# Two strided value groups formed together in seven half-sized products, in a hybrid decoder layer on one core

## The chip, the cores and the metric

The kernel runs on one core of one Trainium2 chip. The metric is the device time of one execution in microseconds (us); below, TensorE is the matrix engine (PE in the profile, PEld its weight loads), VectorE is DVE, ScalarE is ACT, GpSimd is POOL and SyncE is SP. Engines run their own instruction streams strictly in order and wait for each other by semaphores. DMAs are issued by SP (loads of weights) and by POOL (sums of weights in DRAM, and small loads).

## The reference

One decoder layer on 512 tokens of width 1024. An input projection gives queries, keys and values for three token mixers; the branches are gated, merged, projected and normalised, and an MLP with a gated per-layer embedding follows. The part that the change touches is the value projection of the third mixer, dilated attention, with three groups of four heads of width 128:

```python
DIL_PAIRS = ((128, 1), (512, 4), (2048, 16))          # (window, dilation)
proj = x @ w_in                                       # dl_v: 1536 columns, 512 for each group
...
def to_strided(a):
    a = jnp.pad(a, ((0, 0), (0, Lp * dilation - S), (0, 0), (0, 0)))
    a = a.reshape(B, Lp, dilation, H, dh).transpose(0, 2, 3, 1, 4)
    return a.reshape(B, dilation, H, nb, n, dh)
...
o = jnp.einsum('brhcqk,brhckd->brhcqd', prob.astype(vb.dtype), vb)
```

Groups 1 and 2 (dilations 4 and 16) read keys and values by stride. In the kernel both are worked residue by residue modulo 4: residue c holds the 128 tokens c, c+4, c+8, ... (group 2 masks what is not a multiple of 16 away). So their values are wanted in four tiles of 128 tokens by residue.

## The kernel before

**Number format.** Every large product is taken in three passes on float32 data: an operand is split into a high half (a cast on ScalarE) and a low half (the rest, a subtraction on VectorE), and TensorE adds high x high, high x low and low x high. In mm3 (lines 86 to 89) and in v_items (lines 340 to 342) that is three matmuls for each 128-deep slice k.

**Blocks.** Weights come in blocks of 128x1024 (512 KB). fill (line 163) issues their loads on SP into seven raw buffers (`raw`); split_next (line 198) casts a block into `wh` (line 212) and subtracts into `wl` (line 214). RING = 7 (line 135) is the number of split blocks that can stand ready; a block's buffer comes free when the products that read it are done. pump runs this ahead of the products.

**Items.** The program is a list of items, one PSUM bank of products each (`mm`) with an evacuation (`ev`). main_order (line 36) sets their order; the loop at line 1658 walks it: before an item it evacuates the one before, pumps blocks, calls step, which advances the attention generators (sb_head, dil_head, da_block) by a stage, and lets sum_steps issue some DMAs. A scheduler then sets the final order on each engine from these dependencies; the streams shown below as "order" are its result.

**Values of the strided groups.** v_items (line 329) makes a group's 512 columns of values: four items, one for each 128 consecutive tokens, x as the stationary operand (the weights of a load), the weight block as the moving one, 8 slices k x 3 = 24 matmuls each. Groups 1 and 2 were in line at head index 1. Their results are copied into two borrowed raw blocks, and 32 transfers on SP (line 367) gather every fourth row into tiles by residue; after LAND = 6 steps they are handed to the heads.

**Heads.** dil_head, one for each head slot: logits of group 0 (line 1496) and of the strided groups (line 1512), table sums with a running maximum on VectorE (lines 1499 and 1520), exponentials on ScalarE (1505, 1527), a small exchange of maxima and denominators between token order and residue order (r0 and r1, folds at lines 1537 and 1539, sel to mxx), scaling (1561, 1565), transposes (1577, 1586), and the products with the values (1598, 1603). Heads 0 and 1 start one behind the other during the value items.

**Half-sized products elsewhere.** The gate and MLP products already use seven products of halved operands instead of eight. Sums of their weight blocks are formed in DRAM by POOL's DMAs, eight steps a set (up_steps, line 806; plain copy 825, adding copy 823), four sets in turn, from item 16 on at a rate of 1.6 steps an item. Sums of x for the gates are formed by mixer_forms (line 408).

Of the kernel before, what the change touches and what calls it, by code (L numbers as in the profile page):

```python
# [10 lines left out]
F32 = mybir.dt.float32  # L11
# [7 lines left out]
P = 128  # L19
# [16 lines left out]
def main_order():  # L36
# [19 lines left out]
def trunk(tc, a, out):  # L56
    nc = tc.nc
    es = ExitStack()
    with es:
# [7 lines left out]
        NSLOT = 42  # L67
# [67 lines left out]
        RING, RAW = 7, 7  # L135
# [184 lines left out]
        by = {}  # L320
        LAND = 6

        def by_residue(g):
            for _ in range(LAND):
                yield
            for c in range(4):
                V["dl_v", g, c] = by[g][c]

        def v_items(nv, name, g):
            blocks = [{"src": None, "w": 1024, "uses": 2, "own": False} for _ in range(2)]  # L330
            if name == "dl_v" and g > 0:
                items[-2]["blocks"] = blocks
            cs = [chunk(a["wv"][nv, c].rearrange("p k n -> p (k n)"), 1024) for c in range(4)]
            for tt in range(4):
# [11 lines left out]
                def ev(ps, tt=tt):  # L346
# [8 lines left out]
                    elif g == 0:  # L355
# [3 lines left out]
                    else:  # L359

                        b = blocks[tt // 2]
                        t = b["raw"][:, (tt % 2) * 512:(tt % 2) * 512 + 512]
                        cp(t, ps)
                        if tt == 0:
                            by[g] = [slot(name) for _ in range(4)]
                        for c in range(4):
                            nc.sync.dma_start(by[g][c][32 * tt:32 * tt + 32, :], t[c::4, :])
                        b["uses"] -= 1
                        if tt == 3:
                            pending.append(by_residue(g))  # L370
# [5 lines left out]
        for kind, name, j in order[2:]:  # L376
# [5 lines left out]
            else:  # L382
                v_items(nv, name, j)
# [17 lines left out]
        HB = slice(0, 256)  # L401
        HC = slice(256, 512)
# [5 lines left out]
        def mixer_forms():  # L408

            r = {}  # L410
            for h in range(2):
                for th in range(2):
                    for kp in range(2):
                        t = slot("xr")
                        i = nc.gpsimd.dma_start(t.rearrange("p (k t) -> p k t", k=2),
                                                xt[:, 4 * h + 2 * kp:4 * h + 2 * kp + 2, 256 * th:256 * th + 256])
# [1429 lines left out]
```

## Time and profile before

| | us |
|---|---|
| median of 3 runs (1063.29 to 1063.46) | 1063.42 |
| the profiled execution | 1063.83 |
| its span, from first to last instruction | 1062.1 |
| TensorE busy in it | 1050.6 |
| VectorE busy | 750.0 |
| ScalarE busy | 558.5 |

How to read it: a busy share is an average over stages with different limits. Matmuls overlap, so the duration of one in the profile is longer than the distance from its start to the next one's start; the latter is what a matmul costs in a stream. A row of a timeline shows start, duration, engine, line, operation, output<-inputs, shape and count, and in brackets how long the engine was idle before and what released it. A row of a window table shows the stretch, its length, then the busy time (and number of instructions) of TensorE, its weight loads, VectorE, ScalarE and POOL, the granted TensorE clock, the DMA engines' share and their GB/s.

### The profile page before, as it was taken

To read this page: it belongs to the slowest core of one execution; us is meant where nothing else is said; L and a number is where in the kernel's file an instruction comes from. 1 tells how busy PE (TensorE), PEld (TensorE's weight loads), DVE (VectorE), ACT (ScalarE), POOL (GpSimd) and SP (SyncE) were. 2 spreads that over 40 slices of the span, in tenths; PEclk is the share of its full clock that TensorE was granted. 3 is DMA by queue.
4 is the path that set the end of the run, shared out by engine and by line. 5 is a ranking of instruction groups with operands and counts; after the bars stand their busy time and mean duration, and the time that the engine had idled before them with its cause. 6 is when DMAs were issued, how large, how long until landed. Compare 5 with 4: busy or idle time off the path is not lost.

```text
span 1062.1 us, 15599 instructions
## 1 busy us (share of the span) xinstructions
PE 1050.6 (99%) x5826; PEld 904.5 (85%) x5826; DVE 750.0 (71%) x1345; ACT 558.5 (53%) x975; POOL 130.1 (12%) x200
## 2 busy tenths in 40 slices
PE   9999999999999999999999999999999999999996
PEld 6888788888888888888999988888999989989885
DVE  6888667548253757768777773888777877877965
ACT  6666545525232546547545452675766665665741
POOL 0000402021121102230111030101110010000000
PEclk9999999999999999999999999999999999999999
DMA  8433656395896819773766583149989688867502
GB/s 314 134 130 99 210 149 168 140 297 135 315 245 193 235 38 316 153 244 98 200 180 202 175 290 137 67 138 268 269 282 276 235 239 255 259 229 244 189 14 79
DMA packets 60987, 208.21 MB, mean 196 GB/s; under 512 B 7944, under 2 KB 8856, under 8 KB 60912
## 3 DMA queue, kind: packets, MB, share of 16 engines
q1 hardware_dynamic: 37728, 125.76, 34.0%
q0 software_dynamic: 22608, 80.55, 29.4%
q8 instruction: 45, 0.74, 0.3%
q10 hardware_dynamic: 576, 0.92, 0.2%
q14 instruction: 30, 0.25, 0.1%
HBM read 202.97 MB, written 73.42 MB: 260 GB/s over the span
## 4 chain that ended last, share of the span: by engine, by line
PE 88%; DVE 7%; issue 2%; ACT 2%; DMA 0%; POOL 0%; SPq 0%; DVEq 0%; POOLq 0%
PE mm L87 13%; PE mm L89 13%; PE mm L88 13%; PE at L87 4%; PE at L983 4%; PE at L984 4%; PE at L985 4%; PE at L88 4%; PE at L89 4%; PE mm L340 3%; PE mm L342 3%; PE mm L341 3%; DVE wl L214 2%; PE at L131 1%; PE at L312 1%
## 5 line engine op out<-in xcount | busy, mean ns | idle before, releaser
L212 ACT CAST wh<-raw 128x1024 fp32r<-128x1024 f32 (+1 forms) x243 | 250.5, 1034 | 253.7 <-PE mm L88 154.5
L214 DVE TENSOR_TENSOR wl<-raw,wh 128x1024 fp32r<-128x1024 f32 (+1 forms) x243 | 291.5, 1205 | 109.8 <-ACT wh L212 106.4
L87 PE MATMUL mm<-xhT,wh 128*128 128x512 f32 x368 | 146.8, 399 | 0.0
L89 PE MATMUL mm<-xhT,wl 128*128 128x512 f32 x368 | 144.4, 392 | 0.0
L88 PE MATMUL mm<-xlT,wh 128*128 128x512 f32 x368 | 144.1, 392 | 0.0
L89 PEld LDWEIGHTS mm<-xhT,wl 128*128 128x128 f32 x368 | 69.1, 188 | 15.0 <-DVE wl L214 0.3
L87 PEld LDWEIGHTS mm<-xhT,wh 128*128 128x128 f32 x368 | 69.2, 188 | 13.6 <-issue 0.4
L88 PEld LDWEIGHTS mm<-xlT,wh 128*128 128x128 f32 x368 | 69.2, 188 | 13.1
L983 PE MATMUL at<-wh,hh 128*128 128x512 f32 x188 | 73.7, 392 | 0.0
L984 PE MATMUL at<-wl,hh 128*128 128x512 f32 x188 | 73.7, 392 | 0.0
L87 PE MATMUL mm<-x1hT,wh 128*128 128x256 f32 x256 | 73.6, 288 | 0.0
L985 PE MATMUL at<-wh,hl 128*128 128x512 f32 x188 | 73.1, 389 | 0.0
L88 PE MATMUL mm<-x1lT,wh 128*128 128x256 f32 x256 | 72.3, 283 | 0.0
L89 PE MATMUL mm<-x1hT,wl 128*128 128x256 f32 x256 | 71.8, 283 | 0.0
L340 PE MATMUL mm<-wh,xhT 128*128 128x512 f32 x160 | 63.4, 396 | 0.0
L342 PE MATMUL mm<-wh,xlT 128*128 128x512 f32 x160 | 62.5, 391 | 0.0
L341 PE MATMUL mm<-wl,xhT 128*128 128x512 f32 x160 | 62.4, 390 | 0.0
L823 POOL DMA_DIRECT2D usum<-in_wu_dram x32 | 28.0, 874 | 232.8 <-DVE wl L214 199.4
L87 PEld LDWEIGHTS mm<-x1hT,wh 128*128 128x128 f32 x256 | 48.8, 190 | 4.7 <-ACT up L917 2.7
L88 PEld LDWEIGHTS mm<-x1lT,wh 128*128 128x128 f32 x256 | 48.8, 191 | 1.5
L89 PEld LDWEIGHTS mm<-x1hT,wl 128*128 128x128 f32 x256 | 48.6, 191 | 0.0
L823 POOL DMA_DIRECT2D dsum<-in_wd_dram x28 | 26.1, 930 | 139.1 <-DVE wl L214 134.8
(437 smaller groups left out, 2538.4 us busy)
## 6 DMA issues: line engine op xcount, KB each, us to landing
usum<-in_wu_dram POOLq DMA_DIRECT2D x48, 512.0 KB, 8.8
raw<-in_wt_dram SPq DMA_DIRECT2D x46, 512.0 KB, 5.7
dsum<-in_wd_dram POOLq DMA_DIRECT2D x42, 512.0 KB, 9.1
raw<-usum SPq DMA_DIRECT2D x32, 512.0 KB, 6.4
raw<-dsum SPq DMA_DIRECT2D x28, 512.0 KB, 4.7
raw<-in_wd_dram SPq DMA_DIRECT2D x25, 512.0 KB, 4.4
raw<-in_wu_dram SPq DMA_DIRECT2D x24, 512.0 KB, 6.1
raw<-in_wv_dram SPq DMA_DIRECT2D x20, 512.0 KB, 5.0
```

The source lines that it names most:

```text
L87: nc.tensor.matmul(ps, wh, xh, start=start, stop=False, skip_group_check=True)
L88: nc.tensor.matmul(ps, wh, xl, start=False, stop=False, skip_group_check=True)
L89: nc.tensor.matmul(ps, wl, xh, start=False, stop=stop, skip_group_check=True)
L212: i = nc.scalar.copy(h, raw)
L214: i = nc.vector.tensor_sub(lo, raw, h.bitcast(F32))
L340: nc.tensor.matmul(ps, x1, c["h"][:, s], start=k == 0, stop=False)
L341: nc.tensor.matmul(ps, x1, c["l"][:, s], start=False, stop=False)
L342: nc.tensor.matmul(ps, x2, c["h"][:, s], start=False, stop=k == 7)
L823: i = nc.gpsimd.dma_start(o, i, accum_op=OP.add, max_dma_last_dim=4096)
L983: nc.tensor.matmul(ps, h[:, q], c["h"][:, s], start=go, stop=False, skip_group_check=True)
L984: nc.tensor.matmul(ps, h[:, q], c["l"][:, s], start=False, stop=False, skip_group_check=True)
L985: nc.tensor.matmul(ps, lo[:, q], c["h"][:, s], start=False, stop=end, skip_group_check=True)
```

## The change

The values of groups 1 and 2 are formed together, as one product of the 512 tokens by the 1024 inputs by 2 x 512 columns, with every dimension halved: the tokens by residue (residues 0 and 1 against 2 and 3), the inputs into their first and second 512, the columns by group. Seven products of halves (numbered 2, 1, 7, 6, 4, 5, 3 in their order) replace eight. Each has two items, one for each of two residues r, with 4 slices k x 3 = 12 matmuls, so 14 items of half size instead of 8 whole ones.

```diff
-            if h == 1:
+            if h == 1 and g == 0:
                 o += [("V", "dl_v", g)]
+        if h == 2:
+            o += [("V", "dl_v", 1), ("V", "dl_v", 2)]
...
-        NSLOT = 42
+        NSLOT = 46
...
-        RING, RAW = 7, 7
+        RING, RAW = 6, 7
...
+        vf = {p: [[(xh[k][:, 2 * th + r::4], xl[k][:, 2 * th + r::4]) for r in range(2)] for k in range(ks, ks + 4)]
+              for p, ks, th in ((1, 0, 0), (2, 4, 0), (3, 4, 1))}
+        vsum = [[dram.tile([P, 1024], F32, name=f"vsum{m}_{i}") for i in range(4)] for m in range(2)]
...
+        def value_forms():
+
+            xr = [slot("xr") for _ in range(8)]
+            for k, t in enumerate(xr):
+                i = nc.gpsimd.dma_start(t, xt[:, k, :])
...
+            def blk(kh, k, th):
+                return xr[4 * kh + k].rearrange("p (t c) -> p c t", c=4)[:, 2 * th:2 * th + 2, :]
...
+            for _ in range(WAIT):
                 yield
+            f7, o7 = new()
+            with tc.issue_after(st["low"]):
+                for k in range(4):
+                    nc.vector.tensor_sub(o7[k], blk(1, k, 1), blk(0, k, 1))
+            parts(7, f7)
+            yield
+            f6, o6 = new()
+            with tc.issue_after(st["low"]):
+                for k in range(4):
+                    neg_sub(o6[k], o7[k], blk(0, k, 0))
+            yield
+            parts(6, f6)
+            yield
+            f1, o1 = new()
+            for k in range(4):
+                nc.vector.tensor_sub(o1[k], blk(0, k, 0), blk(0, k, 1))
+            yield
+            f4, o4 = new()
+            for k in range(4):
+                neg_sub(o4[k], o6[k], blk(1, k, 0))
+            yield
+            parts(4, f4)
+            yield
+            parts(5, f1)
+            yield
...
+        def value_pair(nv):
+            v_from[0] = len(items) - 4
...
+            for p in (2, 1, 7, 6, 4, 5, 3):
+                for r in range(2):
+                    if not r:
+                        blk = {1: 0, 2: 2, 4: 6}.get(p)
+                        cs[p] = [chunk(vsum[kp][{5: 0, 6: 1, 7: 2, 3: 3}[p]] if blk is None else w[blk + kp], 1024)
+                                 for kp in range(2)]
+
+                    def bank(p=p, r=r):
+                        if p == 5:
+                            x[r] = at_bank()
+                        return x[r] if p in (5, 3) else at_bank() if r else mm_bank()
+
+                    def mm(ps, p=p, r=r):
+                        for k in range(4):
+                            c = cs[p][k // 2]
+                            n = slice(k % 2 * 512, k % 2 * 512 + 512)
+                            h, lo = vf[p][k][r]
...
+                    def ev(ps, p=p, r=r):
+                        if p in (2, 7):
+                            s[p, r] = slot("dl_v")
+                            nc.scalar.copy(s[p, r], ps)
+                        elif p == 1:
+                            s[1, r] = slot("dl_v")
+                            nc.vector.tensor_add(s[2, r], s[2, r], ps)
+                            nc.scalar.copy(s[1, r], ps)
+                            V["dl_v", 1, r] = s[2, r]
+                        elif p == 6:
+                            nc.vector.tensor_add(s[1, r], s[1, r], ps)
+                            nc.vector.tensor_add(s[7, r], s[7, r], s[1, r])
+                        elif p == 3:
+                            nc.vector.tensor_add(s[1, r], s[1, r], ps)
+                            V["dl_v", 1, 2 + r] = s[1, r]
+                        else:
+                            o = V["dl_v", 2, r + 2 * (p == 5)] = slot("dl_v") if p == 4 else s[7, r]
+                            nc.vector.scalar_tensor_tensor(o, s[7, r], -1.0, ps, op0=OP.mult, op1=OP.subtract)
+                    item(cs[p] if r else [], mm, ev, need=cs[p], bank=bank, size=0.5)
...
-                        for c in range(4):
-                            nc.sync.dma_start(by[g][c][32 * tt:32 * tt + 32, :], t[c::4, :])
...
-            todo = deque(up_steps(gsum[m], a["wg"][m]) for m in range(2))
+            w = a["wv"].rearrange("g c p k n -> g c p (k n)")
+            todo = deque(up_steps(vsum[m], [w[2 + i // 2, i % 2 * 2 + m] for i in range(4)], True) for m in range(2))
+            todo.extend(up_steps(gsum[m], a["wg"][m]) for m in range(2))
...
+            if hd < 2:
+                yield
+                yield
...
-        DA_TABS = 41
+        DA_TABS = 47
...
-        RATES = 1.6, 1.0
+        RATES = 1.8, 1.0
...
-            if 16 <= n < wout_at - 6:
+            if 12 <= n < wout_at - 6:
```

In words: the items come after head index 2 instead of 1. Products 2, 1 and 3 take columns of x four apart as their stationary operand; for products 7, 6, 4 and 5 sums of x are formed on VectorE (256 columns at a time, read four apart and written in the order of residues), then split as u7, u6, u4 and u5. Products 5, 6, 7 and 3 read sums of weight blocks, which POOL's DMAs form in DRAM (vsum, 16 more steps). The results fall out by residue, so the transfers, the borrowed blocks and LAND are gone. Each product reads two blocks, 14 in place of 8. Heads 0 and 1 wait two stages more before their transposes, and the ring of split blocks is six instead of seven.

Where the order of instructions moves. On TensorE, in the values of groups 1 and 2 with heads 0 and 1 among them; before (lines 340 to 342 are the products on xhT and xlT, 1537 and 1539 the folds of r0 and r1, 1577 the transposes of a head's group 0 maps, L):

```order
L342 MATMUL mm_2387<-wh_2170,xlT 128x512
L1537 MATMUL at_2468<-r_494_2424,fold 128x32
L1539 MATMUL at_2468<-r_495_2426,foldT 128x32
L1512 MATMUL at_2495<-dl_k_1920,dl_q_1860 128x128 x4
L1512 MATMUL at_2496<-dl_k_2284,dl_q_2229 128x128 x4
L340 MATMUL mm_2523<-wh_1915,xhT 128x512
...
L1577 MATMUL at_2536<-ident,L_483_2367 128x128 x3
L1577 MATMUL at_2536<-ident,L_484_2368 128x128
L1577 MATMUL at_2543<-ident,L_484_2368 128x128 x3
L1537 MATMUL at_2549<-r_512_2519,fold 128x32
```

and now, from the end of product 6's first half on (lines 426 to 428 are the products, 1673 and 1682 the transposes of heads 0 and 1):

```order
L1682 MATMUL at_2734<-ident,L_493_2384 128x128 x2
L427 MATMUL mm_2762<-wl_2506,u6h_2573 128x512
L428 MATMUL mm_2762<-wh_2505,u6l_2574 128x512
L426 MATMUL mm_2819<-wh_2640,u4h_2691 128x512
L427 MATMUL mm_2819<-wl_2641,u4h_2691 128x512
L428 MATMUL mm_2819<-wh_2640,u4l_2692 128x512
...
L428 MATMUL mm_2819<-wh_2646,u4l_2696 128x512
L1673 MATMUL at_2741<-ident,L_511_2460 128x128 x3
...
L426 MATMUL at_2791<-wh_2499,u6h_2569 128x512
```

The stationary operands are now sums of x as well, and the first half of product 4 stands ahead of head 1's transposes and of the second half of product 6.

On VectorE, before, in the same place (from the negated maximum of head 1 to the second block after head 0's scaling):

```order
L1524 TENSOR_SCALAR nm_2443<-st_2428 128x4
L1561 TENSOR_SCALAR L_483_2367<-L_483_2367,mxx_2476 128x128
L1561 TENSOR_SCALAR L_483_2367<-L_483_2367,mxx_2476 128x256
L1561 TENSOR_SCALAR L_484_2368<-L_484_2368,mxx_2476 128x256 x2
L1565 TENSOR_SCALAR L_485_2369<-L_485_2369,mxx_2476 128x256 x2
L1565 TENSOR_SCALAR L_486_2370<-L_486_2370,mxx_2476 128x256 x2
L98 COPY pt_516_2541<-at_2536 128x512
L1533 TENSOR_TENSOR r_513_2521<-st_2428,exf 128x32
L214 TENSOR_TENSOR wl_2589<-raw_2163,wh_2588 128x1024
```

and now, up to the low halves of product 4's sum of x (u4l; fr are the sums, 216 the low half of a block, 1646 to 1650 head 1's exchange):

```order
L1646 TENSOR_TENSOR ex_2604<-ot_2599,mxx_2602 128x8
L369 SCALAR_TENSOR_TENSOR fr_2657<-fr_2481,xr_2188 128x256
L369 SCALAR_TENSOR_TENSOR fr_2657<-fr_2481,xr_2189 128x256
L100 COPY pt_566_2689<-at_2685 128x384
L1648 TENSOR_TENSOR mxx_2602<-ex_2604,st_2459 128x8
L1649 TENSOR_TENSOR ex_2604<-ex_2604,ot_2599 128x8
L216 TENSOR_TENSOR wl_2713<-raw_2294,wh_2712 128x1024
L1650 TENSOR_TENSOR mxx_2602<-mxx_2602,ex_2604 128x8
L240 TENSOR_TENSOR u4l_2692<-fr_2656,u4h_2691 128x512
L1651 RECIPROCAL mxx_2602<-mxx_2602 128x8
L240 TENSOR_TENSOR u4l_2696<-fr_2657,u4h_2695 128x512
```

Ahead of u4l on VectorE, counted from head 0's first table sum, stand in this order six blocks' low halves, all 16 sums of x, the low halves of u7 and u6 (four), two evacuations, one copy, the table sums of heads 0 and 1, head 0's scaling, and their small steps.

More of the change, by code (lines that the diff above doesn't have):

```diff
@@ L318, in first_item @@
             item([cs[k][0] for k in (0, 1, 3, 5, 7)], mm, ev, bank=lambda: (at_bank(), at_bank()))
[L320 to L324, printed above, removed]
-                yield
-            for c in range(4):
-                V["dl_v", g, c] = by[g][c]
+        HB = slice(0, 256)
+        HC = slice(256, 512)
+        vf = {p: [[(xh[k][:, 2 * th + r::4], xl[k][:, 2 * th + r::4]) for r in range(2)] for k in range(ks, ks + 4)]
+              for p, ks, th in ((1, 0, 0), (2, 4, 0), (3, 4, 1))}
@@ L796, in sum_steps, with up_steps @@
         def sum_steps():
-            def up_steps(sums, w):
-                w = [w[i].rearrange("p k n -> p (k n)") for i in range(4)]
+            def up_steps(sums, w, flat=False):
+                w = [w[i] if flat else w[i].rearrange("p k n -> p (k n)") for i in range(4)]
                 a1, a2, a3, a4 = sums
@@ L1684, in trunk @@
                 tie.clear()
-            loads[st["dma"]:st["dma"]] = it.get("blocks", ())
             if n == 4:
```

84 lines of the change are left out of this document (47 added, 37 removed).

## The prediction

> **What bounds the kernel now.** I read the page first (busy shares, granted clock, chain), then TensorE's own waits, then the timeline of TensorE and of VectorE around the value products of the two strided groups.
>
> ```profile
> span 1062.1 us, 15599 instructions
> PE 1050.6 (99%) x5826; PEld 904.5 (85%) x5826; DVE 750.0 (71%) x1345; ACT 558.5 (53%) x975; POOL 130.1 (12%) x200
> PEclk9999999999999999999999999999999999999999
> PE 88%; DVE 7%; issue 2%; ACT 2%; DMA 0%; POOL 0%; SPq 0%; DVEq 0%; POOLq 0%
> ```
>
> TensorE is busy 99% of the span at full clock, and the chain that ends last is 88% TensorE. A busy share can hide matmuls that merely stand long, so the waits are the check:
>
> ```profile
> PE at L1153 <- DVE zero L1150: 1.3, 1, 1.3
> PE at L1444 <- DVE lg L1439: 0.6, 2, 0.4
> PE at L312 <- ACT wh L212: 0.6, 1, 0.6
> PE at L757 <- DVE sg L772: 0.4, 1, 0.4
> PE at L757 <- DVE sg L766: 0.3, 1, 0.3
> ```
>
> Those are all of them: 3.2 us, none near the values. So a matmul taken away is time taken away, at its pace in the stream, not at its duration. The timeline in the dl_v products gives the pace:
>
> ```profile
> 186.25 0.39 PE L340 MATMUL mm<-wh,xhT 128*128 128x512 f32 x1
> ...
> 190.56 0.39 PE L341 MATMUL mm<-wl,xhT 128*128 128x512 f32 x1
> ```
>
> The second row starts 19 matmuls after the first: 4.31 / 19 = **0.227 us each**; the 0.39 beside them overlaps with the next.
>
> **What is removed.** Two groups x 4 token tiles x 8 k x 3 = 192 matmuls become 7 products x 2 residues x 4 k x 3 = 168, of the same 128x512 shape. The order bears it out: 5608 rows on TensorE become 5583, in which 24 are these. 24 x 0.227 = **-5.45 us**, the whole of what can be gained. The 32 row transfers on SP, the copies into ring blocks and the wait of LAND go too; I cost them at nothing, since no row of TensorE's waits names dl_v: they already lie under the products.
>
> **What is added on VectorE, and where.** Prices, start to start, from the timeline where two heads of the dilated attention (dil_head) run back to back:
>
> ```profile
> 243.30 0.29 DVE L1520 CUSTOM_DVE_ANT_0 L<-at,shf 128x128 f32<-128x128 f32 x1 [0.45 <-PE at L1512]
> ...
> 245.28 0.28 DVE L1499 CUSTOM_DVE_ANT_0 L<-at,shf 128x128 f32<-128x128 f32 x1
> ...
> 246.71 0.17 DVE L1503 TENSOR_SCALAR nm<-st 128x4 f32<-128x4 f32 x1
> ...
> 248.85 0.23 DVE L1543 TENSOR_TENSOR sel<-at,pick 128x64 f32<-128x64 f32 x1 [0.86 <-PE at L1539]
> ...
> 249.83 0.29 DVE L1520 CUSTOM_DVE_ANT_0 L<-at,shf 128x128 f32<-128x128 f32 x1
> ...
> 252.37 1.07 DVE L1561 TENSOR_SCALAR L<-L,mxx 128x128 f32<-128x128 f32 x4
> ...
> 254.40 0.68 DVE L98 COPY pt<-at 128x512 f32<-128x512 f32 x1
> ...
> 256.54 1.21 DVE L214 TENSOR_TENSOR wl<-raw,wh 128x1024 fp32r<-128x1024 f32 x1
> 257.67 0.20 DVE L1545 TENSOR_REDUCE ot<-sel 128x8 f32<-128x32 f32 x1
> ...
> 257.90 0.69 DVE L98 COPY raw<-mm 128x512 f32<-128x512 f32 x1
> 258.50 0.16 DVE L1550 TENSOR_TENSOR mxx<-st,ot 128x8 f32<-128x8 f32 x1
> ```
>
> So the eight table sums of L1520 with their reads take 1.98, the four of L1499 1.43, six small steps from L1543 on 0.98 (0.16 each), the scaling of one head (L1561, L1565) 2.03, the low half of a 1024-wide block 1.13, a 512-wide step 0.60. A 256-wide two-input step lasts 0.42 in
>
> ```profile
> L1357 DVE TENSOR_TENSOR sm<-e 128x256 f32<-128x256 f32 x8 | 3.3, 418 | 0.0
> ```
>
> and its pace is that less the 0.09 by which the others overlap: 0.33. Added in all: 6 more blocks (14 instead of 8) x 1.13 = 6.8; 16 sums of x x 0.33 = 5.3; 8 low halves of the sums x 0.60 = 4.8; 12 evacuations on VectorE instead of 4 = 8 x 0.60 = 4.8. Together 21.7 us, all within the 14 half-sized products (38 us of matmuls), and the order puts heads 0 and 1 among them as well. Before, the same two heads had it like this:
>
> ```profile
> 236.00:262.00 26.00, 26.00 (x147) 22.55 (x146) 19.11 (x93) 13.55 (x41) 3.75 (x6) 1.00 0.50 129
> ```
>
> VectorE (third figure) had 19.1 of 26 us, with TensorE full. There is cover, but not for 21.7 us more.
>
> **The place that decides.** In the order, TensorE takes product 4 of residue 0 (matmuls on u4h, u4l) ahead of product 6 of residue 1; its third matmul needs u4l, which stands on VectorE behind nearly everything else. I count both from the start of the first product (product 2), when head 0's first logits are just done. TensorE's prices for the heads:
>
> ```profile
> 242.21 1.95 PE L1512 MATMUL at<-dl_k,dl_q 128*128 128x128 f32 x16
> 243.99 1.68 PE L1496 MATMUL at<-dl_k,dl_q 128*128 128x128 f32 x8
> 245.32 0.59 PE L340 MATMUL mm<-wh,xhT 128*128 128x512 f32 x1
> ```
>
> TensorE up to that matmul: seven half-products x 12 x 0.227 = 19.07, two matmuls of product 4 0.45, two groups of L1512 (242.21 to 243.99) 3.56, head 1's L1496 1.33, 15 transposes of head 0 and 8 fold matmuls at the 1.78 / 16 = 0.111 of L1512 2.56: **27.0 us**. VectorE up to the first half of u4l, by the order's rows: six blocks 6.78, all 16 sums 5.28, five low halves 3.00, two evacuations and one copy 1.80, the tables of two heads 2 x (1.98 + 1.43) = 6.82, head 0's scaling 2.03, two groups of six small steps 1.96, 16 more small ones x 0.16 = 2.56: **30.2 us**. Product 4 thus waits 3.2 us. Below: with the sums at a quarter of the wide block (0.28) and small steps at 0.10, VectorE needs 28.4 and the wait is 1.4. Above: VectorE itself idles. Its row for head 0's first fold operand waits for four exponentials on ScalarE, priced by L1527 (four, then the next line):
>
> ```profile
> 245.69 0.51 ACT L1527 ACTIVATE L<-L,nm 128x256 f32<-128x256 f32 x1 [3.06 <-DVE nm L1524]
> ...
> 247.68 0.39 ACT L1505 ACTIVATE L<-L,nm 128x128 f32<-128x128 f32 x1
> ```
>
> They take 1.99, while VectorE has some three sums (1.0) to do, and u7l behind it waits for the two casts: up to 1.5 more, 4.7 in all. I take 3.2, the plain sum. TensorE is strictly in order: behind the waiting matmul stand the rest of product 4, head 1's transposes and the second half of product 6, and no later stage gives the time back, since TensorE is the bound there.
>
> Two smaller waits of this kind. Head 0's second fold (r1) stands in the order after two matmuls of product 1, at 2.72 x 2 + 1.78 + 1.33 + 0.22 + 1.78 + 0.45 = 11.0 us. Its operand comes behind u7l, which is priced with
>
> ```profile
> L237 ACT CAST hh<-hid 128x512 fp32r<-128x512 f32 x46 | 27.1, 617 | 0.0
> ```
>
> as tables and a block 2.56, one sum and the negated maximum 0.49, exponentials 1.99, first cast 0.62, two low halves 1.20: 6.9. Then eight table sums to 8.8, the next maximum to 9.0, exponentials 1.99, a small step: 11.2 or a little more. So 0 to 1.0, taken 0.5. Head 1's transposes after product 4 need its scaling, one block and two steps behind u4l: 0 to 0.6, taken 0.3.
>
> **What else moves.** POOL's queue gets 16 steps of vsum and 8 loads of x, SP's 6 loads of blocks more and 32 row transfers less. The last vsum step is the 30th of the round of four, at 1.8 an item from item 12: item 28.7. Its landing is priced by
>
> ```profile
> usum<-in_wu_dram POOLq DMA_DIRECT2D x48, 512.0 KB, 8.8
> 140.00:180.00 40.00, 40.00 (x197) 33.09 (x196) 28.20 (x50) 18.65 (x29) 6.26 (x9) 1.00 0.49 125
> ```
>
> 8.8 us is 1.6 items of 24 matmuls, so it is there at item 30.3; product 3's blocks are loaded 13 blocks ahead (7 raw, 6 split), after item 32. The DMA engines stand at 0.49 of their time there (last but one figure). Cost nothing; were a sum late, SP's queue would stand behind its load and the 13 blocks would cover about one landing. ScalarE gets 16 instructions more and has half its time free; its cast of u4 follows head 1's ex, which VectorE releases, so it comes with the wait above and not on top of it.
>
> A ring of six: the places where VectorE is full are the test.
>
> ```profile
> 700.00:710.00 10.00, 10.00 (x46) 8.28 (x45) 10.00 (x16) 8.56 (x14) 0.00 (x0) 1.00 0.29 106
> 710.00:720.00 10.00, 9.67 (x43) 7.71 (x42) 10.00 (x13) 6.36 (x9) 0.98 (x2) 1.00 0.71 184
> ```
>
> There TensorE's wait (L757, quoted above) is for sg, not for a block. One block fewer in hand brings at most one split, 1.13 us, into the full stretch: 0 to 1.1, taken 0.3, since the number of splits between its start and sg stays.
>
> **Sum.** -5.45 + 3.2 + 0.5 + 0.3 + 0.3 = -1.15 us on a span of 1062.1; the profiled execution (1063.83) has 1.7 around the span, and the median of the runs is 1063.42, so I subtract from that: **1062.3 us**. The bounds give -5.45 + 1.4 = -4.05 to -5.45 + 4.7 + 1.0 + 0.6 + 1.1 = +1.95: 1059.4 to 1065.4. A change under 0.2% (2.1 us: 1061.3 to 1065.5) cannot be told from none.
>
> **Rivals.** *All hidden.* VectorE starts head 0's tables earlier than I count, or TensorE comes to product 4 later, and 3.2 is not met. For it: in the stretch 236 to 262 TensorE was full although VectorE ran without a pause from 249.8 on. Against: the sum above is not close. Time: 1058.0 to 1059.4.
>
> *Slower: loads of x four apart.* Products 2, 1 and 3 take every fourth column of x as their stationary operand, 72 loads; no load in this profile does that.
>
> ```profile
> L340 PEld LDWEIGHTS mm<-wh,xhT 128*128 128x128 f32 x160 | 30.1, 188 | 5.7
> L291 DVE COPY dl_k<-mm 128x512 f32<-128x512 f32 x12 | 8.3, 689 | 25.7 <-PE mm L89 25.7
> ```
>
> A contiguous load lasts 188 ns but one can start every 111 (L1512), and it hides under 227. It decides from the point where a load's pace passes 227 ns, twice today's. At three times (333) it costs 72 x 0.106 = 7.6 us, at four times (444) 72 x 0.217 = 15.6; at twice, nothing. For it: nothing measured. Against: the one access four apart that the profile has, eight of the twelve copies of L291 out of PSUM, goes at 689 ns like a plain one (L98, 0.68 and 0.69). Time: 1062.3 + 7.6 = 1069.9, up to 1077.9.
>
> The Trainium skill (Advanced Engine Details and Errata, Memory Cachelines) says that SBUF is read in lines of 16 bytes, that two hits on a line are needed to absorb the latency, and that a new line for every access is penalised; four float32 apart is exactly a new line each time. By that rule the load would be slower, but it gives no size, and no run here shows it; L291 reads PSUM, for which the same section warns of non-contiguous patterns too, and there the trace does not agree.
>
> *Slower: the sums of x are read four apart on VectorE.* All 16 of them read so and all stand ahead of u4l. At twice the pace they add 16 x 0.33 = 5.3 us, all of it on the path just counted: 1062.3 + 5.3 = 1067.6. The decision point is any excess, as VectorE is already the later of the two. For it: the same gap in the profile. Against: L291 again.
>
> That the change does not take the matmuls away is excluded by the order's count.
>
> **How the numbers follow.** Partly eaten by VectorE (the forecast, 1059.4 to 1065.4): 0.52, of which 0.20 fall below 1061.3 and 0.31 between. All hidden: 0.17. Slow loads: 0.16. Slow sums: 0.15, of which little is below 1065.5. So faster 0.37, same 0.31, slower 0.32. The range leaves out the lowest end of the second case and most of the slow loads: 1058.5 to 1068.0.
>
> **What would show it.** Right: 24 matmuls fewer at 0.227; loads of products 1 to 3 at 188 ns and the products' pace at 0.227; a gap of about 3 us on TensorE before product 4's first low half, released by VectorE's u4l or ScalarE's u4h, with VectorE over 95% busy in the 30 us ahead. Wrong: no gap there (all hidden, near 1058); a pace above 0.25 in products 2, 1 and 3 alone (slow loads); sums of x at 0.6 instead of 0.33; or a wait on a block or a landing of vsum, which I gave nothing.

## The result and the profile after

The changed kernel takes 1066.90 us (median of 7 runs, 1066.53 to 1067.35), the kernel before 1063.37: a ratio of 1.0034, 95% interval 1.0022 to 1.0046. It is slower by 3.5 us; the forecast was 1062.3, faster by 1.1. The profiled execution took 1067.35 us with a span of 1065.6, also 3.5 more than before.

The page of the changed kernel, busy shares and granted clock:

```profile
span 1065.6 us, 15588 instructions
PE 1049.0 (98%) x5802; PEld 905.1 (85%) x5802; DVE 774.1 (73%) x1383; ACT 568.5 (53%) x991; POOL 145.8 (14%) x224
PEclk9999999999899999999999999999999999999999
```

The 24 matmuls are gone (5826 records to 5802). New is one 8 in the row of the clock: TensorE did not run at its full clock in the slice around 270 us. TensorE's waits (total us, times, longest):

```profile
PE mm L426 <- ACT u4h L239: 2.1, 1, 2.1
PE mm L428 <- DVE u4l L240: 1.5, 1, 1.5
...
PE at L1673 <- DVE L L1654: 0.2, 1, 0.2
```

Two waits, 3.6 us together, stand at product 4, where they were forecast; the first is already on the high half, whose cast had to wait for the last sums. TensorE's timeline there (start, duration):

```profile
266.08 0.40 PE L428 MATMUL mm<-wh,u6l 128*128 128x512 f32 x1
268.53 0.50 PE L426 MATMUL mm<-wh,u4h 128*128 128x512 f32 x1 [2.06 <-ACT u4h L239]
268.87 0.40 PE L427 MATMUL mm<-wl,u4h 128*128 128x512 f32 x1
270.78 0.79 PE L428 MATMUL mm<-wh,u4l 128*128 128x512 f32 x1 [1.52 <-DVE u4l L240]
271.38 0.63 PE L426 MATMUL mm<-wh,u4h 128*128 128x512 f32 x1
271.80 0.63 PE L427 MATMUL mm<-wl,u4h 128*128 128x512 f32 x1
...
274.79 0.63 PE L428 MATMUL mm<-wh,u4l 128*128 128x512 f32 x1
275.21 1.31 PE L1673 MATMUL at<-ident,L 128*128 128x128 f32 x7
276.36 0.38 PE L1682 MATMUL at<-ident,L 128*128 128x128 f32 x2
```

Read the starts. Start to start the two gaps are 2.45 and 1.91 us; less the 0.23 that a matmul takes anyway, 3.9 us are lost. Behind them the ten matmuls from 270.78 on take 4.43 us, 0.44 each, where 0.227 is the pace: another 2.2 us. The seven transposes of L1673 then take 1.15 us from start to start of the next group, where the seven of head 0 take 0.68 (258.77 to 259.45 in the same trace): another 0.5. A table of stretches shows why (length, busy TensorE, loads, VectorE, ScalarE, GpSimd, then the granted clock):

```profile
262.34:265.75 3.41, 3.41 (x21) 2.71 (x20) 3.41 (x8) 1.56 (x2) 0.80 (x1) 1.00 0.37 105
265.75:269.17 3.42, 1.36 (x7) 0.58 (x5) 3.42 (x13) 2.97 (x7) 0.00 (x0) 1.00 1.01 250
269.17:272.58 3.41, 1.89 (x5) 1.49 (x5) 3.41 (x8) 0.81 (x2) 1.65 (x2) 0.50 0.74 243
272.58:275.99 3.41, 3.41 (x11) 2.65 (x10) 2.67 (x10) 0.00 (x0) 0.00 (x0) 0.50 1.06 216
275.99:279.40 3.41, 3.41 (x23) 2.99 (x22) 2.35 (x4) 1.68 (x3) 0.00 (x0) 1.00 1.04 263
```

From 269.17 to 275.99 the clock granted was half, in two pieces of 3.41 us, right after a piece in which TensorE was busy 1.36 us. The first wait, 2.06 us, lies wholly in that piece; the second stands in the next one, which is already at half clock, and behind it one more piece follows at half.

The rest lies at the very end. The last matmul starts 1.77 us later than before (1055.53 against 1053.76), the span ends 3.5 us later. Every instruction from the last matmul to the last store has its old distance; what is longer is GpSimd's DRAIN, an instruction of the program's last line, behind which all engines exchange their last semaphores. Rows of that line, before and after (duration in ns, least, median, longest):

```profile
L1842 POOLq DRAIN  x3: 46/102/5681, 1055.7 to 1061.9; - x3
```

```profile
L1939 POOLq DRAIN  x3: 46/102/7396, 1057.4 to 1065.3; - x3
```

It takes 7.40 us instead of 5.68, and all engines wait for it: it ends at 1064.8, and the last store of the output had landed at 1062.2. The sum of the change is then -5.45 (matmuls) + 3.9 (waits) + 2.7 (half clock) + 0.6 (strided loads and small rests, below) + 1.7 (DRAIN) = +3.5. The 0.6 is no measurement of its own; it is what the other terms leave of the 1.77 us by which the last matmul is later.

### The profile page after: what moved, and what is told of

Same layout as the page of the kernel before. It is cut to its first block, busy times and chain, and to the rows that moved or that the text cites. A ratio compares the mean times of both kernels' runs of the same rounds, so it can differ in the third digit from the quotient of the medians.

```text
span 1065.6 us, 15588 instructions
## 1 busy us (share of the span) xinstructions
PE 1049.0 (98%) x5802; PEld 905.1 (85%) x5802; DVE 774.1 (73%) x1383; ACT 568.5 (53%) x991; POOL 145.8 (14%) x224
## 4 chain that ended last, share of the span: by engine, by line
PE 88%; DVE 7%; issue 2%; ACT 2%; DMA 0%; POOL 0%; SPq 0%; DVEq 0%; POOLq 0%; ACTq 0%
PE mm L89 13%; PE mm L91 13%; PE mm L90 13%; PE at L89 4%; PE at L1076 4%; PE at L1077 4%; PE at L1078 4%; PE at L91 4%; PE at L90 4%; DVE wl L216 2%; PE mm L458 2%; PE mm L460 2%; PE mm L459 2%; PE at L133 1%; PE at L1467 1%
## 5 line engine op out<-in xcount | busy, mean ns | idle before, releaser
L214 ACT CAST wh<-raw 128x1024 fp32r<-128x1024 f32 x249 | 256.7, 1035 | 262.8 <-PE mm L90 158.7
L216 DVE TENSOR_TENSOR wl<-raw,wh 128x1024 fp32r<-128x1024 f32 x249 | 298.5, 1205 | 99.1 <-ACT wh L214 96.4
L1078 PEld LDWEIGHTS at<-wh,hl 128*128 128x128 f32 x188 | 35.3, 188 | 7.7
L1076 PEld LDWEIGHTS at<-wh,hh 128*128 128x128 f32 x188 | 35.5, 189 | 6.0
L1077 PEld LDWEIGHTS at<-wl,hh 128*128 128x128 f32 x188 | 35.5, 189 | 5.5
```

The source lines that it names most:

```text
L214: i = nc.scalar.copy(h, raw)
L216: i = nc.vector.tensor_sub(lo, raw, h.bitcast(F32))
L1076: nc.tensor.matmul(ps, h[:, q], c["h"][:, s], start=go, stop=False, skip_group_check=True)
L1077: nc.tensor.matmul(ps, h[:, q], c["l"][:, s], start=False, stop=False, skip_group_check=True)
L1078: nc.tensor.matmul(ps, lo[:, q], c["h"][:, s], start=False, stop=end, skip_group_check=True)
```

## The experiments

Twelve kernels, in three groups: what made TensorE wait and lose its clock; what lengthens the end; what repairs both.

**e1: the sums of x read contiguously.** The products 7, 6, 4 and 5 are then of other tokens' sums.

```diff
-                return xr[4 * kh + k].rearrange("p (t c) -> p c t", c=4)[:, 2 * th:2 * th + 2, :]
+                return xr[4 * kh + k].rearrange("p (c t) -> p c t", c=4)[:, 2 * th:2 * th + 2, :]
```

> The changed kernel, but the 16 sums of x read their operands contiguously instead of four apart; the sums are then of other tokens, so products 7, 6, 4 and 5 are those of another matrix, of the same sizes. Theory: VectorE comes late to u4l, TensorE waits, and the clock falls because TensorE waited. The sums then go at about 0.33 us instead of 0.55, which takes 16 x 0.21 = 3.4 us off VectorE ahead of u4l; the waits of 2.1 and 1.5 us on u4h and u4l shrink to under 1 us together, the granted clock stays 1.00 between 260 and 280 us, and the time is 1066.9 - 2.7 (wait) - 2.8 (half clock) = about 1061.4, or down to 1060. Rival: the clock falls for another reason (the dense half-sized products themselves): the 0.50 stretch stays, and the time is about 1064. Rival: the sums are 0.55 us for another reason than the stride: nothing changes, 1066.9.

1064.28 us (1063.15 to 1065.54), ratio to before 1.0005 (0.9996 to 1.0014). The sums by form, the changed kernel first, then this one (busy us, mean ns):

```profile
L369 DVE SCALAR_TENSOR_TENSOR fr<-fr,xr 128x256 f32<-128x256 f32 x8 | 4.8, 629 | 0.0
L388 DVE TENSOR_TENSOR fr<-xr 128x256 f32<-128x256 f32 x4 | 2.2, 631 | 0.0
```

```profile
L369 DVE SCALAR_TENSOR_TENSOR fr<-fr,xr 128x256 f32<-128x256 f32 x8 | 3.2, 418 | 0.0
L388 DVE TENSOR_TENSOR fr<-xr 128x256 f32<-128x256 f32 x4 | 1.4, 424 | 0.0
```

Reading four apart costs 0.21 us a sum, 3.4 us for the 16: the rival on slow sums had its mechanism right. The waits at product 4 fell by less, from 3.6 to 2.3 us. The two traces show where the rest went: from the start of the first product to u4l VectorE was busy 27.4 us instead of 30.3, but the stretch shrank only from 31.6 to 30.2, since VectorE now idled 2.8 us of it instead of 1.3, for ScalarE's exponentials (1.04 and 0.42 us) and for the last matmul of a product (0.87). The profiled run still had half a clock, but for one piece of 3.41 us (270.24 to 273.65) instead of two. Its ten runs fall into five at 1063.2 to 1063.8 and five at 1064.8 to 1065.5; the mean granted clocks are 0.997 to 0.998 and 0.996, so the same kernel seems sometimes to lose the clock and sometimes not; only one execution of it, of the slower five, has a trace. About 1061.4 was expected: little more than a third of the wait was removed.

**e7: waits put into the kernel before.** Ahead of nine items VectorE copies the last bank 1 to 8 times and adds nothing (0 times the copy) to the item's first stationary.

```diff
+            if n in LATE:
+                junk = slot("junk")
+                for _ in range(LATE[n]):
+                    nc.vector.tensor_copy(junk, prev[1])
+                h = need[0]["h"][:, :P]
+                nc.vector.scalar_tensor_tensor(h, junk[:, :P], 0.0, h.bitcast(F32), op0=OP.mult, op1=OP.add)
```

> The kernel before with nine waits put into its first half, 15 us or more apart: ahead of one item each VectorE copies the last bank 1 to 8 times (0.6 us each) and then adds nothing (0 times the copy) to the item's first stationary, so that TensorE waits for about 1.0, 1.6, 2.2, 2.8, 3.4, 4.0, 5.2 us, and once more 2.2 and 2.8. Same result. Theory: a wait alone halves the clock, from a length between 2 and 4 us on, for 3.4 or 6.8 us; shorter waits cost their length only. Rival: the clock fell in the changed kernel for another reason: 1.00 throughout here.

1105.5 us in its one run. The waits came out of other lengths than planned (VectorE was behind at some places), but they serve: the clock fell to half six times, always for 3.41 or 6.83 us, and always at an edge of one running grid of 3.41 us. The pieces of that grid (same columns as above):

```profile
140.99:144.41 3.42, 1.59 (x5) 0.91 (x6) 3.00 (x6) 0.00 (x0) 0.00 (x0) 1.00 1.05 253
144.41:147.82 3.41, 3.41 (x9) 2.63 (x9) 0.00 (x0) 0.00 (x0) 0.00 (x0) 0.50 0.59 148
...
164.89:168.30 3.41, 2.23 (x14) 1.62 (x14) 3.31 (x8) 1.28 (x3) 0.00 (x0) 1.00 0.00 0
168.30:171.71 3.41, 3.41 (x17) 2.81 (x16) 1.95 (x5) 0.00 (x0) 0.00 (x0) 1.00 0.00 0
...
212.67:216.09 3.42, 2.08 (x9) 1.31 (x7) 2.43 (x5) 0.60 (x1) 0.00 (x0) 1.00 0.06 22
216.09:219.50 3.41, 1.55 (x7) 1.03 (x8) 3.13 (x8) 1.54 (x3) 0.00 (x0) 1.00 0.16 57
219.50:222.91 3.41, 2.55 (x8) 1.55 (x7) 3.38 (x8) 1.46 (x3) 0.00 (x0) 0.50 0.40 151
222.91:226.33 3.42, 3.28 (x8) 2.61 (x9) 3.28 (x9) 1.47 (x3) 0.00 (x0) 0.50 0.00 0
```

A piece in which TensorE was busy 1.59 or 1.55 us is followed by half a clock; one with 2.23 or 2.08 is not; and at half clock a piece with 2.55 keeps it, one with 3.28 ends it. Over the traces of this study (from the first record of the clock, 4 to 7 us after the start, to the last matmul) every piece with 1.55 us or less was followed by half a clock, and none with 1.88 or more. Of the three pieces in between, the one above with 1.59 was, and two at the very end of the program (1.57 in the changed kernel, 1.58 in e9) were not. So a wait alone does it, no products of half size are needed, and the point lies where TensorE stands for something like half of a piece.

The Trainium skill (TensorE: Matmul & The Clock Gate, Part 1: The HAM clock gate) describes this gate: a free-running window of about 3.4 us, half the clock after an idle one, full clock after a busy one. Window and grid agree with these rows. Its section "HAM oscillation — how this bites in real kernels" gives as the rule that no gap on TensorE should be longer than about 3.4 us; that is too mild here, since a single gap of 2.06 us in one piece was enough.

**e2: product 3 ahead of product 4.** Product 3 needs no sums; it gets its own bank, and product 5 is read out twice.

```diff
-            for p in (2, 1, 7, 6, 4, 5, 3):
+            for p in (2, 1, 7, 6, 3, 4, 5):
...
-                        return x[r] if p in (5, 3) else at_bank() if r else mm_bank()
+                        return at_bank() if r or p in (5, 3) else mm_bank()
```

> The changed kernel with product 3, which needs no sum of x, ahead of product 4 instead of last; it then has a bank of its own and product 5 is read out twice (two more steps on VectorE). Same result. TensorE gets 24 matmuls x 0.235 = 5.6 us of work ahead of the first matmul on u4h. Theory: 5.6 us cover the 3.6 us of waiting, the clock stays full, and the time is 1066.9 - 3.6 - 2.8 = about 1060.5. Rival: the wait only moves (a block from a sum of weights that has not landed, or VectorE later still because of the two more steps): a gap before product 3 or 4 stays, over 1063. The DRAIN of GpSimd at the end stays at 7.4 us in either case.

1066.40 us, ratio 1.0029 (1.0018 to 1.0041). The wait on u4h stayed, and the second is now for the low half of a block:

```profile
PE mm L424 <- ACT u4h L239: 2.1, 1, 2.1
...
PE mm L425 <- DVE wl L216: 1.1, 1, 1.1
```

The order of TensorE's instructions tells why: product 4's first matmuls still stand ahead of product 3 and of product 6's second residue. My reading is that these two need one of the six banks that the heads hold, three each, until head 1's transposes are done, while product 4 finds one of the projections' two. So the edit did not do what it was to do, and the next run changes the banks.

**e8: all second residues but those of 5 and 3 in the projections' banks.**

```diff
-                        return x[r] if p in (5, 3) else at_bank() if r else mm_bank()
+                        return x[r] if p in (5, 3) else mm_bank()
```

> The changed kernel with the second residue's products 2, 1, 7, 6 and 4 in the two banks of the projections instead of the six that the heads use. Same result. In TensorE's order product 6 of residue 1 then stands ahead of product 4, which gives 12 matmuls = 2.7 us of cover for u4l; but head 0's transposes now stand ahead of product 7, and head 1's in product 6 of residue 0. Theory: VectorE is short over the whole stretch, so the wait moves to the operands of the transposes: 2 to 4 us in all, and 1064 to 1067. Rival: the bank was what held the order back: the wait falls to about 1 us, the clock stays, about 1061.4.

1068.05 us, ratio 1.0043 (1.0030 to 1.0057), even slower than the change:

```profile
PE mm L426 <- ACT dl_v L437: 2.1, 1, 2.1
PE at L1632 <- DVE r L1626: 1.8, 1, 1.8
```

Product 4 waits no more; head 1's fold waits instead, and behind it product 7's second residue waits for its bank to be emptied. VectorE is short over the whole stretch, so a change in TensorE's order moves the wait along.

**e5: the sums begun sooner.** One number: the form generator pauses for 3 half-items instead of 8.

```diff
-        WAIT = 8
+        WAIT = 3
```

> The changed kernel with the sums of x begun five half-items sooner (the wait of the form generator 3 instead of 8). Same result, same work. x had landed at 224.5 us of the trace, VectorE was busy 3.8 of the 10 us from 225 to 235, and the first sum ran at 240.3. In VectorE's order all 16 sums and the low halves of u7 and u6 then stand ahead of head 0's first tables. Theory: what made TensorE wait is where VectorE's work lies, not its amount: both waits on u4 go, the granted clock stays 1.00, and the time is 1066.9 - 3.6 - 2.8 = about 1060.5 (1060 to 1061.5). Rival: VectorE's amount in the products is too much anyway: a wait of 1 to 2 us turns up at the heads' transposes or a block, 1062 to 1064.

1063.26 us, ratio 0.9998 (0.9989 to 1.0007): 3.6 us better than the change, the same as before. Stretches of the changed kernel and of this one (third pair is VectorE):

```profile
225.00:235.00 10.00, 10.00 (x48) 8.27 (x47) 3.82 (x4) 3.12 (x4) 0.81 (x2) 1.00 0.48 177
...
265.00:275.00 10.00, 6.42 (x21) 4.55 (x20) 10.00 (x30) 3.78 (x8) 1.65 (x2) 0.71 0.91 238
```

```profile
225.00:235.00 10.00, 10.00 (x48) 8.30 (x47) 8.79 (x15) 4.62 (x7) 0.00 (x0) 1.00 0.47 177
...
265.00:275.00 10.00, 8.50 (x48) 6.54 (x47) 8.79 (x28) 4.58 (x10) 1.65 (x2) 1.00 1.04 262
```

The same work, put where VectorE was idle, ends the waits on u4 and keeps the clock. What is left is 1.5 us at head 1's transposes, for its scaling (the row's other 0.2 lies at a later head, where the changed kernel has it too), and 0.3 at head 0's first fold:

```profile
PE at L1673 <- DVE L L1654: 1.7, 2, 1.5
...
PE at L1630 <- DVE r L1623: 0.3, 1, 0.3
```

The wait of 1.5 us did not cost the clock; its piece of the grid:

```profile
267.95:271.36 3.41, 1.97 (x9) 1.31 (x7) 3.34 (x12) 0.41 (x2) 0.00 (x0) 1.00 1.05 315
```

The last matmul is 4.0 us earlier than in the changed kernel. 1060.5 was expected; the rival, a wait of 1 to 2 us at the heads' transposes and 1062 to 1064, is what came, and the two waits are 1.8 of the 2.8 us that are missing.

**e4: the ring alone.** In the kernel before:

```diff
-        RING, RAW = 7, 7
+        RING, RAW = 6, 7
```

> The kernel before with a ring of 6 blocks of split weights instead of 7, nothing else. My prediction gave this 0.3 us (0 to 1.1): 1063.4 to 1064.5, the wait on sg at L757 growing if anything. Rival: a smaller ring costs nothing measurable: 1063.4, the same waits.

1063.17 us, ratio 0.9996 (0.9987 to 1.0005), the wait on sg at L757 as before. The ring costs nothing.

**e3 and e6: what lengthens the DRAIN.** In the kernel before, 24 more GpSimd DMAs of 16 bytes; and its plain copies of weights in fewer, longer rows (the trace has 16 rows of 32 KB a copy).

```diff
+            if 24 <= n < 48:
+                i = nc.gpsimd.dma_start(tiny[0:1, 4 * n:4 * n + 4], a["rel"][0:1, 0:4])
```

> The kernel before, with 24 more GpSimd DMAs of 16 bytes each, whose target nobody reads. In the changed kernel GpSimd's last DRAIN took 7.40 us instead of 5.68, and it issued 202 DMAs instead of 178. Theory: the DRAIN grows with the number of DMAs that GpSimd issued: 7.4 us, and the time is 1063.4 + 1.7 = 1065.1 with the last matmul where it was. Rival: it grows with the bytes or the descriptors: 5.7 us and 1063.4. Rival: it varies from run to run: then the spans of the runs scatter by over 1 us.

1063.73 us, ratio 1.0002 (0.9993 to 1.0011); the DRAIN took 5.97 us.

```diff
+                if not plus:
+                    o, i = (t.rearrange("(q r) n -> q (r n)", r=4) for t in (o, i))
...
-                    i = nc.gpsimd.dma_start(o, i, max_dma_last_dim=4096)
+                    i = nc.gpsimd.dma_start(o, i)
```

> The kernel before with the plain copies among GpSimd's sums of weights written as 32 rows of 16 KB instead of 128 rows of 4 KB; the added ones stay. Same bytes, same count of DMAs, fewer packets on the software queue (22608 before). In the changed kernel there were 2944 packets more and the last DRAIN was 1.71 us longer; with 24 tiny DMAs 768 packets more and 0.29 us. Theory: the DRAIN grows with the packets: it falls by several us and the time with it, to 1060 to 1062. Rival: it grows with the bytes: 5.7 us as before, 1063.4. A third reading, that it depends on the DMAs near the end only, gives no change either.

1076.12 us, ratio 1.0125 (1.0110 to 1.0141), mostly by waits elsewhere (5.9 us at one fold of a dilated head, with two pieces of half clock behind it) that I did not follow. The DRAIN took 6.86 us, although the software queue moved the same bytes in 14992 packets instead of 22608. With e3, where 24 DMAs more added only 0.29 us, this leaves none of the three, DMAs, packets or bytes, that sets it alone.

**e9, e10, e11: repairs on top of e5.** e9 gives head 1 two more pauses ahead of its transposes; e10 also has ScalarE issue the 16 loads of x; e11 also the 16 loads of xn and of the norms' factors.

```diff
             if hd < 2:
                 yield
                 yield
+                if hd == 1:
+                    yield
+                    yield
...
-                i = nc.gpsimd.dma_start(t, xt[:, k, :])
+                i = nc.scalar.dma_start(t, xt[:, k, :])
```

> The kernel of the sooner sums with two more half-items of pause in head 1 ahead of its transposes; the second residue of product 6 and of product 4 then stand ahead of them in TensorE's order (24 matmuls instead of 12). Same result. In the run of the sooner sums the last wait in the products was 1.5 us at head 1's transposes (L1673), for the scaling on VectorE. Theory: 2.7 us more of matmuls ahead of them cover it: 1063.3 - 1.6 = about 1061.7, nothing of TensorE's waits left in the products. Rival: the value products of head 1 or a bank come late instead: 1063.3.

1062.58 us, ratio 0.9992 (0.9983 to 1.0000), where 1061.7 was expected. The wait at head 1's transposes fell only to half, from 1.5 us to 0.75:

```profile
PE at L1676 <- DVE L L1654: 0.9, 2, 0.8
```

> The same as the run with head 1 later, and the 16 loads of x (8 for the value products, 8 for the mixer) are issued by ScalarE instead of GpSimd, which is left with 186 DMAs instead of 202 (178 in the kernel before). Same result. GpSimd's last DRAIN was 5.68 us at 178, 7.40 at 202, 5.97 at 202 with 24 tiny ones, 6.86 at 178 with half of the copies in 16 rows. Theory: it follows from what GpSimd's DMAs were, whatever the exact law; with 16 of them gone it changes, to about 6.3 if linear between 178 and 202, and the time by -1.1. Rival: ScalarE's issues (0.15 to 0.35 us each) delay the casts and the time rises by 0.5 or more.

1060.53 us, ratio 0.9974 (0.9964 to 0.9984), DRAIN 5.97 us, 1.43 less. The time fell by 2.05; where the other 0.6 comes from is not shown.

> The same as the run before it, and 16 more loads (8 of xn, 8 of the norms' factors) issued by ScalarE: GpSimd is left with 170 DMAs. Same result. Theory: the DRAIN goes under the 5.68 us of the kernel before (about 5.1 if linear) and the time with it, to about 1059.5 to 1060.5. Rival: ScalarE waits for the slots of these loads, and TensorE for ScalarE: a wait of a us or more appears at the end of the output projection.

1060.69 us, ratio 0.9973 (0.9962 to 0.9983), DRAIN 4.71 us; no wait for ScalarE over 0.2 us. The DRAIN is 1.26 us shorter again, but the time did not follow: it now ends (1057.84 in the trace) just as the last store of the output lands (1057.83). Both beat both kernels: 2.7 us under the runs of the kernel before beside them, and over 6 under the changed one.

**e12: the kernel before with its own 24 such loads issued by ScalarE.** The same replacement at three places, nothing of the change.

> The kernel before with its 24 loads of x for the mixer, of xn and of the norms' factors issued by ScalarE instead of GpSimd: 154 GpSimd DMAs instead of 178, nothing of the change. Same result. This prices the last DRAIN apart from the change. Theory: 0.08 to 0.09 us a DMA (7.39 at 202, 5.97 at 186, 4.71 at 170 in the last three runs) gives 5.68 - 24 x 0.084 = 3.7 us and 1063.35 - 2.0 = about 1061.4; the changed kernel with sooner sums, later head and 32 such loads moved (1060.7) is then 0.7 us better by the products alone. Rival: the DRAIN does not fall here: 1063.35, and the whole 2.7 us belongs to the change so mended.

1062.67 us, ratio 0.9994 (0.9985 to 1.0003), not clear of no change; the median is 1.0 under that of the runs beside it. The DRAIN fell as expected, to 3.44 us, the time less than half as far:

```profile
L1842 POOLq DRAIN  x3: 46/102/3442, 1055.4 to 1060.7; - x3
```

It now ended at 1058.8, before the last store of the output landed (1060.0), which sets the end instead. All DRAINs together:

```
kernel                                  GpSimd DMAs   DRAIN, us   last matmul to end of span
before (and e4, e7)                         178         5.68        8.4 (before)
after (and e1, e2, e5, e8, e9)              202         7.39-7.40  10.1 (after)
e3: before + 24 of 16 bytes                 202         5.97        8.7
e6: before, 68 copies in longer rows        178         6.86        9.6
e10                                         186         5.97        8.6
e11                                         170         4.71        7.7
e12                                         154         3.44        7.6
```

## Why the prediction was wrong, point by point

**Right: the matmuls.** 24 records fewer, each worth 0.227 us in the stream: -5.45.

**Right: the place and the mechanism of the wait; its size partly by luck.** 3.2 us (1.4 to 4.7) were forecast at product 4; 3.9 were measured, 3.6 by the list of waits. Both counts behind it were short, by 2.0 and 1.3 us, and so the difference held. VectorE had the first half of u4l ready at 270.6, 32.2 us after the first product began (238.38), not 30.2: the sums went at 0.55 us instead of 0.33 (+3.4), the rest took 1.4 less than counted. The term of 5.28 us for the 16 sums was thus mis-sized (8.7); the rival that gave them a higher price had its mechanism right. With the price of the forecast, in e1, the waits are 2.3 us and not 3.2. TensorE came to product 4 at 266.31, 27.9 after the start, where the count gave 26.6.

**Put at nothing: the strided loads of x.** They were given no cost unless their pace passed 227 ns. It did, barely. One line of the loads of each kind (busy us, mean ns, idle us before):

```profile
L427 PEld LDWEIGHTS at<-wl,xhT 128*128 128x128 f32 x16 | 5.0, 312 | 0.0
...
L427 PEld LDWEIGHTS at<-wl,u5h 128*128 128x128 f32 x8 | 1.5, 188 | 0.3
```

A load four apart lasts 312 ns instead of 188. The matmuls of products 2, 1 and 3 start 0.235 us apart, 72 x 0.008 = 0.6 us, and at three places the first of a group behind a head's small matmuls comes 0.21 late, where a contiguous one came 0.09 late before: 0.4 more. I estimate 1.0 us from these; 0.6 is left in the sum, with small gains elsewhere (the wait for the first block is 0.4 instead of 0.6). The rival with its 7.6 to 15.6 us is out. I had argued from the copies of L291 that access four apart is free; those read PSUM, and the two readers of SBUF here pay more, TensorE's loads two thirds (312 against 188 ns), VectorE's sums half in duration (629 against 418) and two thirds in pace (0.55 against 0.33).

The Trainium skill's rule on lines of 16 bytes (Advanced Engine Details and Errata, Memory Cachelines), cited in the prediction, has the right sign on both.

**The first step that failed: a wait was priced at its length.** The sum took 3.2 us of waiting as 3.2 us. But the first of the two waits, 2.06 us in one piece of the clock's grid, halved the clock, the second came at half clock, and the 6.8 us of half clock cost 2.7 us: 2.2 of matmuls and 0.5 of transposes. e7 shows it without any product, e5 shows that with shorter waits the clock stays. A row that could have warned me is in the trace of before: the first nine matmuls of the program, 128x512 each, take 4.02 us, 0.447 each, twice the pace. (They are bf16, on zeros, and no granted clock is on record so early; that they ran at half clock is my reading.)

**The second: "What else moves" put POOL's 24 DMAs at nothing.** I looked at where they land and at who waits for the data, and not at the end of the program, where GpSimd's DRAIN runs and everybody waits. They cost 1.7 us there. e10 and e11 show the other direction: the DRAIN is 1.43 us shorter without 16 loads of x, and 1.26 shorter again without 16 of xn and the norms' factors. The time followed the first (-2.05) and not the second, where the last store had become as late.

**The small terms.** Head 0's second fold (0.5) did not wait, nor did head 1's transposes (0.3) behind the slow matmuls: the 0.2 us in the list of waits lie at a later head, 358 us into the trace, where the kernel before has 0.1. The ring (0.3) costs nothing (e4). No block and no sum of weights was late.

From the forecast's -1.15 to the measured +3.5 it is thus 0.7 more of waiting at product 4, 1.1 less for the small terms, 0.6 for loads and rests, 2.7 of half clock and 1.7 of DRAIN. Without the two failed steps the time would be 1066.9 - 2.7 - 1.7 = 1062.5, close to the forecast of 1062.3, but only because the smaller errors cancel. The steps are not independent: the measured time lies inside the stated range, whose upper end stood for slow sums, and e1, with quick sums, is 2.6 us under the changed kernel by the medians, 1.3 of it waiting and some 0.9 half clock (an estimate: one piece of 3.41 us instead of two). The slow sums thus made the wait long enough to cost the clock for longer, but even without them the time stays 2.0 us above the forecast.

What the change is worth once mended is read from e11 against e12, both with their loads on ScalarE, each by the runs beside it: 2.65 against 1.02 us by the medians, 0.27% against 0.06% by the ratios, so some 1.6 to 2.2 of the 5.45. The last matmuls of the two traces are 2.2 us apart. The two kernels did not run side by side, so this is an estimate.

Left open: what exactly the DRAIN counts. A DMA of 16 bytes added 0.012 us, one of 256 KB with 128 rows 0.08 to 0.09, longer rows made it longer, not shorter. Also not shown is why e6 waits at the fold, where the last 0.75 us of head 1's wait in e9 could be hidden, and whether the two times of e1 are the grid's doing, as its mean clocks suggest.

## What to carry to other kernels

A wait on a TensorE that never pauses costs its length only while it is short: add up what TensorE stands within one piece of 3.4 us, and once that nears half of it (1.5 us in e5 did not matter, 2.06 in the changed kernel did), price the half clock that follows as well. When work is added to an engine with spare time, ask in which ten microseconds the time is spare; here the kernel took 3.6 us less when the same 16 sums started at 224 instead of 240 us. And follow every DMA that is added to GpSimd to the end of the program: its last DRAIN grew with most of them, and loads that need no adding are better issued elsewhere, down to the point where the last store sets the end.

## What the runs showed of the hardware

- TensorE's clock is granted in pieces of 3.41 us on a running grid. 1.55 us or less of busy TensorE in a piece meant half a clock in the next, 1.88 or more did not, and between 1.57 and 1.59 both occurred; at half clock 2.55 did not restore it and 3.28 did. Where the grid lies against the program differs from trace to trace (its first edge on record is 4.0 to 7.0 us after the start), which is probably why e1 has two times.
- A stationary load four float32 apart lasts 312 ns instead of 188, and hides under 227 ns of matmul almost entirely (0.235 from start to start). A two-input step on VectorE of 128x256 with its inputs four apart lasts 629 ns instead of 418.
- GpSimd's last DRAIN lasted 3.4 to 7.4 us, to within 0.003 us the same in every kernel with the same GpSimd DMAs (5.681 in three traces, 7.394 to 7.396 in six).
